# Normalising attention by a reciprocal row read back from memory instead of a broadcast made on TensorE

## The chip, the cores and the metric

The kernel runs on one core of a Trainium2 chip. The metric is the device time of one execution in microseconds (us); of several runs the median is given. PE is TensorE, DVE is VectorE, ACT is ScalarE, POOL is GpSimd and SP is SyncE, whose queue issues all transfers of this kernel.

## What is computed

One inference step of a two-layer backbone. Layer 0 runs multi-head latent attention beside a convolution branch; layer 1 is a bidirectional Mamba-2 mixer. Two groups of tokens go through both: 256 context tokens, which see only themselves, and 1024 latent tokens, which see 512 cached context tokens and all 1024 latent ones. The change touches attention alone, and of it the last steps:

```python
s = (einsum('bqhd,bkhd->bhqk', qn, k_nope) + einsum('bqhr,bkr->bhqk', qr, k_rope)) * ATTN_SCALE
p = softmax(s, axis=-1)
out = einsum('bhqk,bkhd->bqhd', p, v)          # 8 heads, 64 wide each
...
mix = concatenate([attn, cv], axis=-1) * silu(gate)
return mix @ w_out, ckv, k_rope
```

The kernel leaves softmax unnormalised until the values are multiplied, so it owes each query a factor 1/(sum of its exponentials), beside the gate.

## The kernel before

Attention runs by **units** (p, b, j, qi): p is one of 4 pairs of heads, b one of 5 blocks of 256 queries (b=0 is context with 256 keys, b=1 to 4 are latent with 1536 keys), j the head of the pair, qi the half of the block (128 queries). 80 units follow each other in that order; four units with the same (p, b) are called a **group** here, 20 in all, numbered 0 to 19, and units are numbered 0 to 79.

For each unit `u_scores` makes 128 x 1536 scores on PE into three PSUM banks (tile `pss`, three float32r products for each, lines 119 to 121), takes their row maximum on DVE (`mx`, `nm`, lines 617 and 621), and exponentiates on ACT (`prob`, line 626), which also leaves the sums. DVE adds the sums and takes the reciprocal, one column of 128 numbers (`ri`, lines 630, 631 and 633). `u_trans`, called one unit later, transposes `prob` on PE, four blocks of 128 x 128 to a bank (`pspt`, line 646), and copies them to `ptile` on ACT (line 652) or DVE (line 650). When a group's four units are through, `u_values` multiplies values by `ptile` into one PSUM bank (`pspo`, line 666), head j=0 into partitions 0 to 63 and j=1 into 64 to 127. A unit has 3 x 3 matmuls of scores, 12 transposes, and a quarter of 24 matmuls of values (for b=0: 3, 2, and a quarter of 4).

The reciprocal has one number per query, and queries lie along the free side of `pspo`; it must reach all 64 partitions of its head. Before, PE did that: a matmul of `ri`, repeated over 64 columns, with the identity puts the row into the right half of the same bank, four such matmuls a group (line 661). DVE then makes the gate times that row (`t2`, line 671, printed as `t` in the profile) and the product with the values (`om`, line 672), and SP stores `om` to memory (`mixd`, line 673). The gate `sg` is loaded from memory (line 705), two buffers.

A scheduler orders each engine's instructions after the program is recorded, so what is written in one function may stand among instructions of other units; each engine, SP too, runs its own list strictly in order. Between the units stand the normalisation of the convolution branch (`conv_norm`) and the keys and queries of the next pair (`prep_pair`, after units 19, 39 and 59). From unit 68 on, `load_mix` reads `mixd` back (line 690) and splits it on ACT (line 691) and DVE (line 692) into `hl` for the output projection, eight rows of heads k in the order 4, 5, 6, 7, 0, 1, 2, 3. Row k=3 needs the last pair's blocks b=0 to 2, that is group 17. The output projection (tile `psmm`) follows the last group.

Of the kernel before, what the change touches and what calls it, by code (L numbers as in the profile page):

```python
# [10 lines left out]
F32 = mybir.dt.float32  # L11
# [3 lines left out]
AF = mybir.ActivationFunctionType  # L15
# [35 lines left out]
def body(nc, tc, d, dbg=None, stop=None):  # L51
    es = ExitStack()
    with es:
        _body(nc, tc, d, es, dbg or {}, stop)


def _body(nc, tc, d, es, dbg, stop):
    V, S, G, PE = nc.vector, nc.scalar, nc.gpsimd, nc.tensor
    dma = nc.sync.dma_start

    def pool(name, bufs=1, space=None, side=None, stack=es):
        kw = {}
        if space is not None:
            kw["space"] = space
        if side is not None:
            kw["side"] = side
        if space is None:
            kw["reuse_waits"] = "tile"
        return stack.enter_context(tc.tile_pool(name=name, bufs=bufs, **kw))
# [5 lines left out]
    sm = pool("sm", bufs=3, side="left")  # L75
# [9 lines left out]
    dp = pool("dp", space=DRAM)  # L85

    def psum(tag="x"):
        tag = tag if tag in ptags else "sd"
        p, n = ptags[tag]
        return p.tile([128, 512], F32, name="ps" + tag, tag=tag, bufs=n)  # L90
# [5 lines left out]
    ident = cp.tile([128, 128], F32, name="ident")  # L96
# [21 lines left out]
    def mm3(ps, lh, ll, rh, rl, start, stop_):  # L118
        PE.matmul(ps, lh, rh, start=start, stop=False)  # L119
        PE.matmul(ps, lh, rl, start=False, stop=False)  # L120
        PE.matmul(ps, ll, rh, start=False, stop=stop_)  # L121

    def after(ins, other):
        tc.add_manual_dep(ins.ins, other.ins.name,
                          mybir.DependencyInfo(mybir.DependencyClass.Sync, mybir.DependencyReason.DATA), reason="group")
# [56 lines left out]
    def bcast_cols(r, j0, jn, ps):  # L182
        for j in range(jn):
            PE.matmul(ps[:, j * 128:(j + 1) * 128], r[:, j0 + j:j0 + j + 1].to_broadcast([128, 128]), ident,
                      start=True, stop=True)
        return ps
# [246 lines left out]
    for c0, n in CHUNKS:  # L433
        ps = psum()
# [65 lines left out]
    ap_ = pool("attn", bufs=2, side="right", stack=esB)  # L500
# [20 lines left out]
    for c0, n in CHUNKS:  # L521
        ps = bcast_cols(rq, c0 // 128, n // 128, ps=psum("pt"))
# [69 lines left out]
    units = []  # L592
    for p in range(4):
        for b in range(5):
            for j in range(2):
                for qi in range(2):
                    units.append((p, b, j, qi))

    def u_scores(u, kq):
        p, b, j, qi = u  # L600
        ks, qs = kq
        tok = (0 if b == 0 else 256 + 256 * (b - 1)) + 128 * qi
        ci = 0 if tok < 256 else (1 if tok < 768 else 2)
        o = tok - CHUNKS[ci][0]
        segs = [0] if b == 0 else [1, 2, 3]
        qh, ql = qs[(j, ci)]
        mx = sm.tile([128, 4], F32, name="mx", tag="mx", bufs=6)
        sums = sm.tile([128, 4], F32, name="sums", tag="sums", bufs=6)
        nk = sum(KSEG[si][1] for si in segs)
        prob = ap_.tile([128, 1536], F32, name="prob", tag="prob")  # L610
        pss = []
        for x, si in enumerate(segs):
            n = KSEG[si][1]
            kh, kl = ks[(j, si)]
            ps = psum("s")
            mm3(ps[:, :n], qh[:, o:o + 128], ql[:, o:o + 128], kh[:, :n], kl[:, :n], True, True)
            V.tensor_reduce(mx[:, x:x + 1], ps[:, :n], axis=AX.X, op=ALU.max, negate=len(segs) == 1)  # L617
            pss.append((ps, n))
        if len(segs) > 1:
            nm = sm.tile([128, 1], F32, name="nm", tag="nm", bufs=6)  # L620
            V.tensor_reduce(nm, mx[:, :len(segs)], axis=AX.X, op=ALU.max, negate=True)  # L621
        else:
            nm = mx[:, 0:1]
        c = 0
        for x, (ps, n) in enumerate(pss):
            S.activation(prob[:, c:c + n], ps[:, :n], AF.Exp, bias=nm, accum_out=sums[:, x:x + 1])  # L626
            c += n
        ri = sm.tile([128, 1], F32, name="ri", tag="ri", bufs=8)
        if len(segs) > 1:
            V.tensor_reduce(ri, sums[:, :len(segs)], axis=AX.X, op=ALU.add)  # L630
            V.reciprocal(ri, ri)
        else:
            V.reciprocal(ri, sums[:, 0:1])
        return prob, ri, nk

    def u_trans(u, st, pts):
        p, b, j, qi = u
        prob, ri, nk = st
        for g in range(0, nk // 128, 4):
            n4 = min(4, nk // 128 - g)  # L640
            if qi == 0:
                pts[(j, g)] = ap_.tile([128, 4, 256], F32, name="ptile", tag="pt", bufs=7)
            dst = pts[(j, g)]
            ps = psum("pt")
            for x in range(n4):
                PE.transpose(ps[:, x * 128:(x + 1) * 128], prob[:, (g + x) * 128:(g + x + 1) * 128], ident)  # L646
            o = dst[:, :n4, qi * 128:qi * 128 + 128]
            p3 = ps[:, :n4 * 128].rearrange("p (k q) -> p k q", q=128)
            if g == 4:
                V.tensor_copy(o, p3)  # L650
            else:
                S.copy(o, p3)  # L652
        pts[("r", j, qi)] = ri

    def u_values(p, b, pts):
        q0 = 0 if b == 0 else 256 + 256 * (b - 1)
        kts = list(range(2)) if b == 0 else list(range(2, 14))
        po = psum("po")
        for qi in range(2):
            for j in range(2):  # L660
                PE.matmul(po[64 * j:64 * j + 64, 256 + 128 * qi:384 + 128 * qi],
                          pts[("r", j, qi)].to_broadcast([128, 64]), ident, start=True, stop=True)
        for x, kt in enumerate(kts):
            for j in range(2):
                h = 2 * p + j
                PE.matmul(po[64 * j:64 * j + 64, 0:256], vt[:, kt, 64 * h:64 * h + 64],  # L666
                          pts[(j, 4 * (x // 4))][:, x % 4, :], start=x == 0, stop=x == len(kts) - 1)
        t2 = ap_.tile([128, 256], F32, name="t2", tag="t2")
        sg = sgs.pop((p, b))
        om = ap_.tile([128, 256], F32, name="om", tag="om")  # L670
        V.tensor_mul(t2, sg, po[:, 256:512])
        V.tensor_mul(om, po[:, 0:256], t2)
        dma(mixd[p, :, q0:q0 + 256], om)

    KORD = (4, 5, 6, 7, 0, 1, 2, 3)
# [9 lines left out]
    def load_mix(gi, ks):  # L685
        g0, gn, _ = GRP[gi]
        for k in ks:
            hi = gtile(gi, "hl", F32R, p=hls[gi])
            lo = gtile(gi, "hl", F32R, p=hls[gi])
            dma(f32(lo), mixd[k, :, g0:g0 + gn])  # L690
            S.copy(hi, f32(lo))
            V.tensor_sub(lo, f32(lo), f32(hi))
            mix[gi][0][k], mix[gi][1][k] = [(g0, hi)], [(g0, lo)]
# [1 line left out]
    state = {}  # L695
    kqs = {0: prep_pair(0)}
    done, ci, sgs = {}, 0, {}
    late_v = []
    cn = [st for t0 in range(0, T, 256) for st in [conv_norm(t0)] * 5]
    for i in range(len(units) + 2):  # L700
        if i < len(units):
            u = units[i]
            if i % 4 == 0:
                sgs[u[:2]] = ap_.tile([128, 256], F32, name="sg", tag="sg")
                dma(sgs[u[:2]], sgd[u[0], :, 256 * u[1]:256 * u[1] + 256])
            state[u] = u_scores(u, kqs[u[0]])
            if i % 20 == 19 and u[0] < 3:
                kqs[u[0] + 1] = prep_pair(u[0] + 1)
        if 0 < i <= len(units):
            v = units[i - 1]  # L710
            pts = done.setdefault((v[0], v[1]), {})
            u_trans(v, state.pop(v), pts)
            if v[2] == 1 and v[3] == 1:
                late_v.append(v)
        if i % 4 == 1 and late_v:
            v = late_v.pop(0)
            u_values(v[0], v[1], done.pop((v[0], v[1])))
        if ci < len(cn) and i % 20 in (1, 3, 5, 7, 9, 11, 13):
            next(cn[ci])
            ci += 1  # L720
        if i == 68:
            esE.close()
            esA.close()
            wps[0] = pool("wpB", bufs=2, side="left")
            hls.append(pool("hlB0", bufs=16, side="left", stack=esH))
            load_mix(0, KORD[:4])
            wao.extend(split_w(d["wao"][m], 8, 128) for m in range(2))
    assert ci == len(cn)
    esB.close()
    esP.close()  # L730
    dump("mix", mixd.rearrange("a p t -> (a p) t"))
# [157 lines left out]
    def dtile(name, dt=F32, tag=None):  # L889
        return dq.tile([128, HT], dt, name=name, tag=tag or name)  # L890
# [40 lines left out]
    p = dtile("p")  # L931
# [43 lines left out]
    for half in range(2):  # L975
        hs = slice(half * 64, half * 64 + 64)
        for c0 in range(0, 5):
            c = half * 5 + c0
            ps = psum("sd")
# [560 lines left out]
```

## Time and profile before

| | |
|---|---|
| three runs | 2059.69, 2059.83, 2062.99 us (median 2059.83) |
| profiled execution, its own time | 2060.95 us |
| its span | 2059.1 us |
| PE busy over the span | 1993.4 us (97%) |
| DVE busy | 1415.9 us (69%) |
| ACT busy | 882.3 us (43%) |
| attention's units | about 380 to 797 us |

The page's busy shares are averages over stages with different limits, so the stage of attention is read by itself: how busy each engine is in stretches of it, which instructions follow each other on PE and at what distance, and which waits stand at the place where the change puts new ones. Times in the views are counted from the start of the span.

### The profile page before, as it was taken

What the parts mean: (1) busy time and instruction counts of PE and PEld (TensorE: products, weight loads), DVE (VectorE), ACT (ScalarE), POOL (GpSimd) and SP (SyncE); (2) the same over time, 40 slices, a digit from 0 to 9 for tenths busy, and PEclk for the clock granted to TensorE, in tenths of its full rate; (3) what the DMA queues carried; (4) which work ended last, traced back from release to release, by engine and by line L of the source; (5) the groups of instructions that cost most, each with busy time, mean ns of one, the idle gap of its engine ahead of it and who ended that gap; (6) DMA issues with size and microseconds to landing.
All of it is one profiled execution on the core that took longest, in us unless ns stands there. A gap on an engine that the chain in (4) does not pass through costs nothing.

```text
span 2059.1 us, 32474 instructions
## 1 busy us (share of the span) xinstructions
PE 1993.4 (97%) x11830; PEld 1626.0 (79%) x11830; DVE 1415.9 (69%) x2257; ACT 882.3 (43%) x1683; POOL 578.7 (28%) x487
## 2 busy tenths in 40 slices
PE   6999999999999999989999999999999999799997
PEld 3787888777777777868888888888888888589997
DVE  5798798556666673275757876876778587784744
ACT  5411321666566673244544343443334244333531
POOL 1211122212222311563123333333433243342001
PEclk8999999999999999999999999999999999999998
DMA  8434213311122224331566768765866678755442
GB/s 315 181 118 150 54 70 108 115 57 42 57 60 60 77 82 164 140 114 52 142 217 205 229 203 237 208 191 173 244 204 194 179 235 252 220 182 185 145 157 72
DMA packets 273341, 313.57 MB, mean 152 GB/s; under 512 B 21184, under 2 KB 221920, under 8 KB 273184
## 3 DMA queue, kind: packets, MB, share of 16 engines
q1 hardware_dynamic: 273184, 311.51, 48.0%
q8 instruction: 94, 1.54, 0.3%
q14 instruction: 63, 0.52, 0.1%
HBM read 223.38 MB, written 88.05 MB: 151 GB/s over the span
## 4 chain that ended last, share of the span: by engine, by line
PE 90%; DVE 3%; DMA 2%; ACT 1%; issue 1%; SPq 1%; POOL 0%; DVEq 0%; ACTq 0%; POOLq 0%
PE psmm L119 18%; PE psmm L120 18%; PE psmm L121 18%; PE pspo L666 5%; PE pspt L646 4%; PE pssd L1078 3%; PE pss L119 3%; PE pssd L1159 3%; PE pss L121 3%; PE pss L120 3%; PE pssd L1164 2%; PE pssd L1136 2%; PE pssd L1139 2%; PE psx L229 1%; PE pstm L1036 1%
## 5 line engine op out<-in xcount | busy, mean ns | idle before, releaser
L119 PE MATMUL psmm<-hl,wh 128*128 128x512 f32 (+1 forms) x1152 | 428.1, 372 | 4.7 <-ACT wh L114 3.5
L121 PE MATMUL psmm<-hl,wl 128*128 128x512 f32 (+1 forms) x1152 | 423.5, 368 | 4.3 <-POOL wl L115 4.3
L120 PE MATMUL psmm<-hl,wh 128*128 128x512 f32 (+1 forms) x1152 | 423.3, 367 | 0.0
L115 POOL TENSOR_TENSOR wl<-ws,wh 128x1024 fp32r<-128x1024 f32 x89 | 223.6, 2514 | 516.7 <-ACT wh L114 424.5
L119 PEld LDWEIGHTS psmm<-hl,wh 128*128 128x128 f32 x1152 | 219.1, 190 | 37.6 <-ACT wh L114 4.5
L121 PEld LDWEIGHTS psmm<-hl,wl 128*128 128x128 f32 x1152 | 218.8, 190 | 36.9 <-POOL wl L115 6.2
L120 PEld LDWEIGHTS psmm<-hl,wh 128*128 128x128 f32 x1152 | 218.8, 190 | 29.6 <-issue 0.7
L383 DVE SCALAR_TENSOR_TENSOR cacc<-cvin,acw,cacc 128x1295 f32<-128x1295 f32 x120 | 206.9, 1740 | 4.6 <-ACT cacc L378 3.1
L114 ACT CAST wh<-ws 128x1024 fp32r<-128x1024 f32 x109 | 113.6, 1043 | 199.6 <-PE psmm L120 140.3
L848 DVE SCALAR_TENSOR_TENSOR cy<-raw,prm,cy 128x1282 f32<-128x1282 f32 x96 | 157.2, 1637 | 24.6 <-ACT cy L845 17.0
L120 PE MATMUL psmm<-hlo,wh 128*128 128x512 f32 (+3 forms) x480 | 172.1, 359 | 0.0
L119 PE MATMUL psmm<-hh,wh 128*128 128x512 f32 (+3 forms) x480 | 167.8, 360 | 2.5 <-ACT hh L259 2.0
L121 PE MATMUL psmm<-hh,wl 128*128 128x512 f32 (+3 forms) x480 | 170.1, 357 | 0.0
L617 DVE TENSOR_REDUCE mx<-pss 128x1 f32<-128x512 f32 (+1 forms) x208 | 137.3, 668 | 35.2 <-PE pss L121 34.2
L1083 POOL TENSOR_TENSOR st<-st,dec_bc 128x256 f32<-128x256 f32 x104 | 84.3, 815 | 245.2 <-DVE st L1085 165.9
L119 PE MATMUL psmm<-yh,wh 128*128 128x256 f32 (+1 forms) x476 | 147.8, 314 | 5.2 <-ACT yh L1203 3.1
L120 PE MATMUL psmm<-yl,wh 128*128 128x256 f32 (+1 forms) x476 | 148.0, 312 | 0.4 <-DVE yl L1204 0.4
L121 PE MATMUL psmm<-yh,wl 128*128 128x256 f32 (+1 forms) x476 | 147.1, 313 | 0.0
L626 ACT ACTIVATE prob<-pss,nm 128x512 f32<-128x512 f32 x192 | 130.3, 693 | 16.1 <-DVE nm L621 14.2
L646 PE MATMUL pspt<-ident,prob 128*128 128x128 f32 x800 | 121.7, 278 | 4.9 <-ACT prob L626 3.9
L652 ACT COPY ptile<-pspt 128x512 f32<-128x512 f32 (+1 forms) x144 | 81.2, 569 | 104.8 <-PE pspt L646 104.0
L646 PEld LDWEIGHTS pspt<-ident,prob 128*128 128x128 f32 x800 | 92.1, 141 | 40.4 <-ACT prob L626 10.2
(337 smaller groups left out, 4084.5 us busy)
## 6 DMA issues: line engine op xcount, KB each, us to landing
xa<-cmb SPq DMA_DIRECT2D x80, 384.0 KB
wm<-in_wmod_dram SPq DMA_DIRECT2D x48, 512.0 KB
ws<-in_wc_dram SPq DMA_DIRECT2D x40, 512.0 KB
eb<-eyd SPq DMA_DIRECT2D x160, 128.0 KB
ws<-in_wco_dram SPq DMA_DIRECT2D x32, 512.0 KB
cmb<-xt SPq DMA_DIRECT2D x24, 640.0 KB
bx<-cmb SPq DMA_DIRECT2D x72, 192.0 KB
eb<-cmb SPq DMA_DIRECT2D x80, 128.0 KB
```

The source lines that it names most:

```text
L114: S.copy(wh, ws)
L115: (eng or G).tensor_sub(wl, ws, f32(wh))
L119: PE.matmul(ps, lh, rh, start=start, stop=False)
L120: PE.matmul(ps, lh, rl, start=False, stop=False)
L121: PE.matmul(ps, ll, rh, start=False, stop=stop_)
L383: V.scalar_tensor_tensor(cacc[i], cv[:, k:k + CO], acw[:, 31 * i + k:31 * i + k + 1], cacc[i], ALU.mult, ALU.add)
L617: V.tensor_reduce(mx[:, x:x + 1], ps[:, :n], axis=AX.X, op=ALU.max, negate=len(segs) == 1)
L626: S.activation(prob[:, c:c + n], ps[:, :n], AF.Exp, bias=nm, accum_out=sums[:, x:x + 1])
L646: PE.transpose(ps[:, x * 128:(x + 1) * 128], prob[:, (g + x) * 128:(g + x + 1) * 128], ident)
L666: PE.matmul(po[64 * j:64 * j + 64, 0:256], vt[:, kt, 64 * h:64 * h + 64], pts[(j, 4 * (x // 4))][:, x % 4, :], start=x == 0, stop=x == len ...
L848: V.scalar_tensor_tensor(y, raw[:, k:k + RO], ccw[:, 5 * blk + k:5 * blk + k + 1], y, ALU.mult, ALU.add)
L1083: G.tensor_mul(n.rearrange("p (h e) -> p h e", e=64), s.rearrange("p (h e) -> p h e", e=64), dec_ap(u, dr, c))
```

## The change

PE's four matmuls a group with the identity go, and so does the product of gate and row. In their place:

- the four reciprocals of a group go into the four columns of one tile `ri` [128, 4], and after the fourth unit SP stores it to memory, to a row of `rid` [20, 4, 128], transposed by the store's addresses (2 KB, in runs of one number of 4 bytes);
- `u_values` multiplies the values in PSUM by the gate and leaves the product in `om` (three buffers instead of two);
- at the first unit of the next group but one (unit 4g+8 for group g) `row_load` reads the row back, twice, once for each head, each time repeated to 64 partitions (`rb`, two buffers); a dependency makes it wait for the last exponential recorded by then, that of unit 4g+8;
- two units later `row_scale` multiplies `om` by `rb` on DVE, and SP stores `om` to `mixd`.

```diff
+    rgs, late_o, last_exp = {}, deque(), []
+    rid = dp.tile([20, 4, 128], F32, name="rid")
...
-        ri = sm.tile([128, 1], F32, name="ri", tag="ri", bufs=8)
+        if (j, qi) == (0, 0):
+            rgs[p, b] = sm.tile([128, 4], F32, name="ri", tag="ri", bufs=4)
+        ri = rgs[p, b][:, 2 * j + qi:2 * j + qi + 1]
...
-        return prob, ri, nk
+        last_exp[:] = [ex]
+        if (j, qi) == (1, 1):
+            dma(rid[5 * p + b].rearrange("c q -> q c"), rgs.pop((p, b)))
+        return prob, nk, mx
...
-        for qi in range(2):
-            for j in range(2):
-                PE.matmul(po[64 * j:64 * j + 64, 256 + 128 * qi:384 + 128 * qi],
-                          pts[("r", j, qi)].to_broadcast([128, 64]), ident, start=True, stop=True)
...
-        V.tensor_mul(t2, sg, po[:, 256:512])
-        V.tensor_mul(om, po[:, 0:256], t2)
+        om = ap_.tile([128, 256], F32, name="om", tag="om", bufs=3)
+        V.tensor_mul(om, po[:, 0:256], sgs.pop((p, b)))
+        late_o.append((p, b, q0, om))
+
+    def row_load(it):
+        rb = ap_.tile([128, 256], F32, name="rb", tag="rb")
+        for x in range(2):
+            ld = dma(rb[64 * x:64 * x + 64], rid[5 * it[0] + it[1], 2 * x:2 * x + 2].rearrange("c q -> (c q)")
+                     .unsqueeze(0).to_broadcast([64, 256]))
+            if last_exp:
+                after(ld, last_exp[-1])
+        return rb
+
+    def row_scale(it, rb):
+        p, b, q0, om = it
+        V.tensor_mul(om, om, rb)
         dma(mixd[p, :, q0:q0 + 256], om)
...
-    for i in range(len(units) + 2):
+    for i in range(len(units) + 7):
...
+        if i % 4 == 0 and late_o:
+            rows_.append((late_o[0], row_load(late_o.popleft())))
+        if i % 4 == 2 and rows_:
+            row_scale(*rows_.popleft())
```

Three places show what the scheduler makes of it. The first is PE in the middle of attention, around units 13 and 14 (`prob_3517` and `prob_3506` are unit 13 before and now, `prob_3600` and `prob_3581` unit 14). Before:

```order
L646 MATMUL pspt_3630<-ident_63,prob_3517 128x128 x4
L661 MATMUL pspo_3782<-ident_63,ri_3494 64x128
L646 MATMUL pspt_3636<-ident_63,prob_3517 128x128 x4
L119 MATMUL pss_3655<-kh_2861,qh_2951 128x512
...
L121 MATMUL pss_3699<-kh_2839,ql_2907 128x512
L661 MATMUL pspo_3782<-ident_63,ri_3621 64x128
L661 MATMUL pspo_3782<-ident_63,ri_3538 64x128
L646 MATMUL pspt_3676<-ident_63,prob_3600 128x128 x4
L646 MATMUL pspt_3683<-ident_63,prob_3600 128x128 x4
```

Now:

```order
L654 MATMUL pspt_3610<-ident_63,prob_3506 128x128 x4
L654 MATMUL pspt_3616<-ident_63,prob_3506 128x128 x4
L669 MATMUL pspo_3766<-ptile_3529,vt_2713 64x256
L119 MATMUL pss_3637<-kh_2862,qh_2952 128x512
...
L121 MATMUL pss_3681<-kh_2840,ql_2908 128x512
L654 MATMUL pspt_3651<-ident_63,prob_3581 128x128 x4
L654 MATMUL pspt_3658<-ident_63,prob_3581 128x128 x4
```

The 64-column matmuls of line 661 that stood alone between transposes and scores are gone; a single one of the values (line 669 now) has come forward to stand alone in one such place. Counted over all of attention, stretches of 64-column matmuls between other work on PE go from 109 (37 of them of line 661 alone) to 74.

The second is DVE around the sums of unit 28 (`ri_4425` before, `sums_4373` now; `sums_4420` is unit 29). Before:

```order
L630 TENSOR_REDUCE ri_4425<-sums_4403 128x1
L617 TENSOR_REDUCE mx_4529<-pss_4532 128x1
L621 TENSOR_REDUCE nm_4464<-mx_4446 128x1
L631 RECIPROCAL ri_4425<-ri_4425 128x1
L617 TENSOR_REDUCE mx_4529<-pss_4537 128x1
L630 TENSOR_REDUCE ri_4469<-sums_4447 128x1
```

Now:

```order
L635 TENSOR_REDUCE ri_4395<-sums_4373 128x1
L620 TENSOR_REDUCE mx_4494<-pss_4497 128x1
L624 TENSOR_REDUCE nm_4437<-mx_4419 128x1
L636 RECIPROCAL ri_4395<-ri_4395 128x1
L620 TENSOR_REDUCE mx_4494<-pss_4502 128x1
L686 TENSOR_TENSOR om_4258<-om_4258,rb_4416 128x256
L635 TENSOR_REDUCE ri_4395<-sums_4420 128x1
```

The product with the loaded row of group 5 has come in between, behind the second maximum of unit 30 and ahead of the sums of unit 29; its load waits for the exponential of unit 28.

The third is ACT near the end of attention, at the split of row k=3 of `mixd` (`hl_7514` before, `hl_7435` now). Before, it stood behind unit 74's exponentials (`prob_7125`):

```order
L626 ACTIVATE prob_7125,sums_7124<-pss_7136,nm_7141 128x512
L652 COPY ptile_7082<-pspt_7161 128x4x128
L691 CAST hl_7514<-hl_7515 128x768
L652 COPY ptile_7193<-pspt_7194 128x4x128
L626 ACTIVATE prob_7169,sums_7168<-pss_7170,nm_7185 128x512
```

Now it stands behind unit 77's (`prob_7187`) and ahead of unit 78's (`prob_7260`):

```order
L629 ACTIVATE prob_7187,sums_7186<-pss_7198,nm_7203 128x512
L705 CAST hl_7435<-hl_7436 128x768
L660 COPY ptile_7224<-pspt_7225 128x4x128
L660 COPY ptile_7210<-pspt_7283 128x4x128
L629 ACTIVATE prob_7260,sums_7259<-pss_7261,nm_7276 128x512
```

It has moved three units later, with the store of group 17 that its load reads.

## Rows read from the trace of the kernel before

**Rows 1.** Stretches of attention: length, then busy PE, PEld, DVE, ACT, POOL, then clock.

```profile
440.00:500.00 60.00, 59.19 (x374) 41.88 (x373) 35.82 (x77) 33.18 (x83) 14.18 (x14) 1.00 0.26 75
740.00:790.00 50.00, 48.65 (x320) 34.66 (x320) 35.42 (x77) 36.75 (x89) 0.06 (x1) 1.00 0.24 82
```

**Rows 2.** Chain that ended last, 430 to 470 us, by line.

```profile
by line: PE pspo L666 30.2%; PE pspt L646 27.4%; PE pss L119 14.3%; PE pss L121 12.3%; PE pss L120 12.1%; PE pspo L661 4.0%; issue 0.1%
```

**Rows 3.** Groups by shape, 360 to 830 us: count, busy us, mean ns, idle before.

```profile
L666 PE MATMUL pspo<-ptile,vt 128*64 128x256 f32 x800 | 111.5, 386 | 0.0
...
L661 PE MATMUL pspo<-ident,ri 128*64 128x128 f32 x160 | 25.4, 297 | 0.7 <-DVE ri L631 0.7
...
L671 DVE TENSOR_TENSOR t<-sg,pspo 128x256 f32<-128x256 f32 x20 | 8.4, 421 | 34.7 <-PE pspo L666 34.7
```

**Rows 4.** PE's instructions in order of time, 446 to 466 us: start, duration, line.

```profile
446.91 0.60 PE L646 MATMUL pspt<-ident,prob 128*128 128x128 f32 x4
447.44 0.43 PE L661 MATMUL pspo<-ident,ri 128*64 128x128 f32 x2
447.80 0.66 PE L646 MATMUL pspt<-ident,prob 128*128 128x128 f32 x4
448.21 0.48 PE L119 MATMUL pss<-kh,qh 128*128 128x512 f32 x1
...
450.91 0.44 PE L661 MATMUL pspo<-ident,ri 128*64 128x128 f32 x4
451.28 1.09 PE L646 MATMUL pspt<-ident,prob 128*128 128x128 f32 x8
452.13 0.48 PE L119 MATMUL pss<-kh,qh 128*128 128x512 f32 x1
...
461.94 2.38 PE L666 MATMUL pspo<-ptile,vt 128*64 128x256 f32 x20
464.25 0.66 PE L646 MATMUL pspt<-ident,prob 128*128 128x128 f32 x4
464.83 0.65 PE L666 MATMUL pspo<-ptile,vt 128*64 128x256 f32 x2
465.41 0.50 PE L119 MATMUL pss<-kh,qh 128*128 128x512 f32 x1
```

**Rows 5.** ACT and DVE around the last exponential of unit 28, in order of time.

```profile
518.23 0.25 ACT L626 ACTIVATION_READ_ACCUMULATOR prob<-pss,nm 128x1 f32 x1
...
520.29 0.67 DVE L617 TENSOR_REDUCE mx<-pss 128x1 f32<-128x512 f32 x1
523.31 0.16 DVE L630 TENSOR_REDUCE ri<-sums 128x1 f32<-128x3 f32 x1 [2.35 <-ACT prob L626]
```

**Rows 6.** Store of group 17, load of row k=3 and its split, in order of time.

```profile
758.77 0.34 SPq L673 DMA_DIRECT2D mixd<-om  x1
...
760.75 0.32 SPq L690 DMA_DIRECT2D hl<-mixd  x1
...
764.21 0.87 ACT L691 CAST hl<-hl 128x768 fp32r<-128x768 f32 x1
```

**Rows 7.** Units 76 to 78 on ACT and DVE, in order of time.

```profile
771.01 0.22 ACT L626 ACTIVATION_READ_ACCUMULATOR prob<-pss,nm 128x1 f32 x1
...
773.70 1.38 DVE L617 TENSOR_REDUCE mx<-pss 128x1 f32<-128x512 f32 x2 [2.08 <-PE pss L121]
...
777.21 0.22 ACT L626 ACTIVATION_READ_ACCUMULATOR prob<-pss,nm 128x1 f32 x1
...
782.46 0.69 ACT L626 ACTIVATE prob<-pss,nm 128x512 f32<-128x512 f32 x1
```

**Rows 8.** End of attention, in order of time.

```profile
788.71 0.16 DVE L631 RECIPROCAL ri<-ri 128x1 f32<-128x1 f32 x1
...
796.42 0.42 DVE L672 TENSOR_TENSOR om<-pspo,t 128x256 f32<-128x256 f32 x1
...
796.99 0.36 PE L119 MATMUL psmm<-hl,wh 128*128 128x256 f32 x1 [1.06 <-DVE raw L813]
```

More of the change, by code (lines that the diff above doesn't have):

```diff
@@ L625, in u_scores @@
         for x, (ps, n) in enumerate(pss):
-            S.activation(prob[:, c:c + n], ps[:, :n], AF.Exp, bias=nm, accum_out=sums[:, x:x + 1])
+            ex = S.activation(prob[:, c:c + n], ps[:, :n], AF.Exp, bias=nm, accum_out=sums[:, x:x + 1])
             c += n
-        ri = sm.tile([128, 1], F32, name="ri", tag="ri", bufs=8)
+        if (j, qi) == (0, 0):
+            rgs[p, b] = sm.tile([128, 4], F32, name="ri", tag="ri", bufs=4)
+        ri = rgs[p, b][:, 2 * j + qi:2 * j + qi + 1]
         if len(segs) > 1:
@@ L633, in u_scores @@
             V.reciprocal(ri, sums[:, 0:1])
-        return prob, ri, nk
+        last_exp[:] = [ex]
+        if (j, qi) == (1, 1):
+            dma(rid[5 * p + b].rearrange("c q -> q c"), rgs.pop((p, b)))
+        return prob, nk, mx
     def u_trans(u, st, pts):
         p, b, j, qi = u
-        prob, ri, nk = st
+        prob, nk, _ = st
         for g in range(0, nk // 128, 4):
@@ L652, in u_trans @@
                 S.copy(o, p3)
-        pts[("r", j, qi)] = ri
     def u_values(p, b, pts):
@@ L667, in u_values @@
                           pts[(j, 4 * (x // 4))][:, x % 4, :], start=x == 0, stop=x == len(kts) - 1)
-        t2 = ap_.tile([128, 256], F32, name="t2", tag="t2")
-        sg = sgs.pop((p, b))
-        om = ap_.tile([128, 256], F32, name="om", tag="om")
-        V.tensor_mul(t2, sg, po[:, 256:512])
-        V.tensor_mul(om, po[:, 0:256], t2)
+        om = ap_.tile([128, 256], F32, name="om", tag="om", bufs=3)
[12 more added lines that the diff above has]
+        V.tensor_mul(om, om, rb)
         dma(mixd[p, :, q0:q0 + 256], om)
@@ L697, in _body @@
     done, ci, sgs = {}, 0, {}
-    late_v = []
+    late_v, rows_ = [], deque()
     cn = [st for t0 in range(0, T, 256) for st in [conv_norm(t0)] * 5]
-    for i in range(len(units) + 2):
+    for i in range(len(units) + 7):
         if i < len(units):
@@ L727, in _body @@
             wao.extend(split_w(d["wao"][m], 8, 128) for m in range(2))
-    assert ci == len(cn)
+    assert ci == len(cn) and not late_o and not rows_
     esB.close()
```

## The prediction

> **What bounds the kernel now.** I read the stage first by stretches [rows 1]. In the middle of attention PE is busy 59.19 of 60 us at full clock (the row's 1.00), DVE 35.82 and ACT 33.18; near the end PE has 48.65 of 50. No other engine is near its limit, and PE hardly waits. The chain of waits from 430 to 470 us says the same in another way [rows 2]: every step is PE's own instruction following another one of PE, and line 661 has 4.0% of it. So this stage costs what PE's instructions take from start to start, and I price removed work by these distances, not by durations, which overlap.
>
> The group table shows why durations would mislead [rows 3]: line 661 has 160 instructions (80 matmuls, two each) of 297 ns, 25.4 us busy, but two of them that run beside each other need far less. The same table says that DVE's first product waits 34.7 us in 20 times for PE's last values. DVE is thus late for nobody there; it waits for PE.
>
> **What line 661 costs on PE.** In [rows 4] one matmul of line 661 stands between two times four transposes and then scores: from 446.91 to 448.21 is 1.30 us. Eight transposes in one piece and then scores take 451.28 to 452.13, 0.85 us. That makes 0.45 us for one excursion. Two matmuls in one excursion take 0.37 us (450.91 to 451.28), one takes 0.36 (447.44 to 447.80): the second is nearly free. Coming in costs as well: the four transposes ahead of it take 0.53 us (446.91 to 447.44) where eight take 0.85, that is 0.42 for four. And the first eight transposes behind an excursion are themselves a little slow, so I take 0.48 us each.
>
> In the order of the program there are 37 excursions of line 661 alone (20 with one matmul, 17 with two). They go: 37 x 0.48 = 17.8 us. Of the other 26 matmuls, those that stand with a single matmul of the values run beside it and cost nothing; three places with three of them in front of values cost about 0.36 us each: 1.1 us. Together 18.9 us.
>
> Against that, the values are cut up a little more. Ten matmuls of values take 2.31 us (461.94 to 464.25), one takes 0.58 (464.83 to 465.41) [rows 4]: 0.43 for each two, head by head side by side, plus 0.15 for leaving, and about 0.10 for coming in. There are 74 excursions with values where there were 72 (0.5 us), and because more of them have an odd number, 225 pairs instead of 222 (1.3 us). PE's gain is 18.9 - 1.8 = 17.1 us.
>
> **What comes in its place, on DVE.** The two products on DVE stay two: gate times values reads PSUM as before (0.42 us, [rows 3]), the product with the loaded row reads SBUF. No row has that one alone with this shape; I take 0.42 as well, and between 0.2 and 0.5 it changes nothing, since DVE has 24 us idle in 60.
>
> The question is the wait for `rb`. The load is held back until the last exponential of unit 4g+8 and the product stands on DVE five instructions behind that unit's sums. For group 5 I can put times to it from [rows 5]: ACT ends unit 28 at 518.48. SP then issues two loads at 0.32 us each, and the second lands about 1.98 us after its issue (the nearest row is a store and the load that waited for it, 758.77 to 760.75 [rows 6]; these loads move half as much each). That is about 521.1 to 521.4. DVE has done the second maximum of unit 30 at 520.96, so it waits 0.2 to 0.4 us and multiplies until 521.8; its next instruction waits for unit 29's exponential until 523.31 anyway, with 2.35 us idle before it in the row. The product falls into that hole. The other groups have the same order on DVE; in the three at a change of pairs, where the units are short, the product stands one unit later. I charge 1 us in all for places where a copy or a maximum stands right behind the product; 0 to 6 for the range.
>
> On SP the store of reciprocals and the two loads wait for DVE and ACT, and loads of keys for the next pair, of gates, and stores of `mixd` queue behind them. The keys are wanted only after four short units, and the gates four units later. I charge nothing; if a load of keys did come late, it would hold PE for a few us at each of three changes of pairs.
>
> The store of the reciprocals consists of numbers of 4 bytes, and no row shows such a store; only the last group waits for it. There the reciprocal is done at 788.87, and the product with the row is wanted at 796.84, when DVE's last product of before ends [rows 8]. With 0.32 and 0.64 us of issuing and 1.98 us for the loads, the store may take up to 5 us before it is late. I take 2 to 4: hidden. Were it late, the output projection would still have three PSUM banks to fill before it needs DVE. The Trainium skill speaks against this store ("DMA: Bandwidth & Descriptors", rules for kernel authors): a transfer whose last dimension is not contiguous is cut into one descriptor for each element, here 512. No run so far shows the price; by it the sum would only change if the store took over 5 us.
>
> PE's first matmul of the projection waits for the release of the values' bank, two products after the last values before, one now: 0.42 us gained [rows 8].
>
> **What the later store costs.** Row k=3 of the mixed input needs the store of group 17, now behind the product at unit 77's maxima instead of right behind its values. At the times of [rows 7] that product ends at about 775.5 (the two maxima end at 775.08). Store 1.98 us and load up to 3.46 us, as in [rows 6], give 780.9. ACT has finished unit 77 at 777.43, and the split stands next in its list: it is idle for 3.5 us, where it would have copied transposes. The split ends at 781.8, DVE's half of it at 782.8; three maxima of 0.69 us come behind that, so unit 78's exponential starts at about 785 instead of 782.46. PE has transposes of unit 77 and scores of 79 to do meanwhile, so not all of it is lost: 2 us, between 0 and 3.
>
> **Sum.** -17.1 (PE) + 1.0 (DVE's waits) + 2.0 (row k=3) - 0.4 (bank) = -14.5 us. The profiled execution took 2060.95 us, 1.1 above the median of the runs: 2046.5 for the profile, 2045.4 in medians. I forecast 2045.5, and 2042 to 2050 for this case.
>
> **Rivals.** (a) The freed time turns into bubbles. PE's list is 4% shorter, but a unit's loop of maximum, exponential, copy and transposes is not, and the scheduler has placed it anew. For it: near the end PE already waits a little [rows 1]. Against it: DVE and ACT have 40% idle. If a unit lost 0.1 us on average, 8 us would go: 2053 (2050 to 2058).
> (b) DVE's wait for `rb` is the new bound. It is one mechanism at one place: the list of DVE, with maxima and copies behind the product. It decides when the row lands later than the next sums are due, 4.8 us after the exponential in [rows 5] instead of my 2.6 to 2.9; SP held up by another wait would do it. If then 18 groups lost 1.5 us each on PE, 27 us would eat the gain: 2060 - 17 + 27 = 2070, slower.
> (c) PE is not the bound; its modelled ends only hide waiting, and then removed matmuls save nothing: 2060. Against it stand the even distances of [rows 4] and a chain without any other engine [rows 2]. The Trainium skill ("Perfetto Trace Analysis", Identifying the Most-Contended Engine) calls a matmul's busy share no good measure and wants that of the weight loads, which is 70% here (41.88 of 60 in [rows 1]); by that rule there would be room on PE, and this rival is what it would give.
> (d) The excursions cost more than I take and the split of k=3 is hidden: -17.1 - 0.4 - 2 = -19.5, 2040.
>
> **How the numbers follow.** Forecast 0.62, (a) 0.16, (b) 0.07, (c) 0.07, (d) 0.08. The range goes down to 2039 for (d) and up to 2056 for most of (a); outside are (b), (c) and the ends, under 2 in 10. About 0.2% (4.1 us) is what a measurement of this kernel tells from no change. Faster by more than that: the forecast, (d), and two thirds of (a), 0.81. Within it: a third of (a) and most of (c), 0.11. Slower: (b) and a rest, 0.08.
>
> **What would show it.** In the profile of after: no line with `ident,ri`; attention's stage from 380 to about 782 instead of 797 us; PE still above 97% busy in its middle; the product with `rb` preceded by less than 0.5 us of waiting for a DMA in most groups; a wait of ACT for the load of `hl` of some 3 us near the end. I would be wrong if DVE shows over 1 us of waiting for `rb` in many groups, if PE's wait for `prob` grows by several us, or if the split of k=3 holds ACT for much longer.

## The result, and the profile after

The changed kernel takes 2095.7 us (median; 2089.7 to 2098.0), the kernel before, beside it, 2061.4. The ratio is 1.0163, with a 95% interval of 1.0147 to 1.0178: 34 us slower, where 15 us faster was forecast, and outside the range. The profiled execution has a span of 2094.1 us.

The loss lies in attention. From its first scores to the first matmul of the output projection it takes 447.5 us instead of 415.3. Stretches of the kernel after, with columns as in [rows 1]:

```profile
440.00:500.00 60.00, 57.77 (x348) 41.67 (x345) 38.00 (x87) 35.82 (x91) 13.96 (x13) 1.00 0.37 74
740.00:790.00 50.00, 43.93 (x264) 30.67 (x263) 29.66 (x66) 30.55 (x71) 7.13 (x3) 0.93 0.37 82
790.00:830.00 40.00, 33.88 (x208) 23.61 (x207) 16.46 (x42) 17.95 (x46) 0.00 (x0) 0.89 0.08 20
```

In the middle PE has lost 1.4 of 60 us against [rows 1], near the end 4.7 of 50, and there the granted clock is 0.93 instead of 1.00. The chain of waits from 430 to 470 us, which had only PE in [rows 2], now has the load of the row as its largest line ("DMA rb<-rid 21.5%"). Some of the waits from 375 to 850 us (engine and line, what it waited for, us in total, times, longest):

```profile
DVE om L686 <- DMA rb<-rid: 76.1, 19, 7.9
ACT hl L705 <- DMA hl<-mixd: 33.4, 6, 17.8
ACT prob L629 <- DVE nm L624: 24.5, 13, 4.3
PEld pss L119 <- ACT prob L629: 20.6, 33, 2.4
PE pss L119 <- ACT prob L629: 9.9, 13, 2.1
DVE om L672 <- PE pspo L669: 6.3, 8, 1.3
```

DVE hardly waits for PE's values any more (34.7 us in [rows 3], 6.3 now). It waits 76.1 us for the loaded row instead, 19 times 4 us on average, and ACT and PE wait behind it. Of the 33.4 us of `hl` only 11.1 lie inside attention (up to 830 us); the rest, with the longest wait, belongs to splits behind attention, where the kernel before waits as well (22.2 us in the same stretch, none of it inside attention). At the product of group 5, which the prediction worked out from [rows 5], SP and DVE show this (start, us, engine and line, what, idle before):

```profile
519.86 0.37 SPq L641 DMA_DIRECT2D rid<-ri  x1
522.36 1.09 SPq L678 DMA_DIRECT2D rb<-rid  x2
...
528.57 0.43 DVE L686 TENSOR_TENSOR om<-om,rb 128x256 f32<-128x256 f32 x1 [4.00 <-DMA rb<-rid]
```

The store at 519.86 is the one of the *next* group, 6. The trace's semaphore events give a landing for each transfer (from its issue to the last increment): this store lands at 528.1, 8.3 us after its issue, and the loads of group 5's row, issued 2.5 us behind it, at 528.5. Over the 20 groups the store takes 8.3 us (median; 7.9 to 10.7) for 2 KB, and the loads 5.9 (2.4 to 9.7). All loads under 2.8 us but one had no store in flight; that one was issued 0.5 us ahead of a store.

The end of attention shows the same, with the projection waiting for it:

```profile
819.30 0.54 SPq L641 DMA_DIRECT2D rid<-ri  x1
...
827.59 0.43 DVE L686 TENSOR_TENSOR om<-om,rb 128x256 f32<-128x256 f32 x1 [6.94 <-DMA rb<-rid]
827.93 0.42 DVE L672 TENSOR_TENSOR om<-pspo,sg 128x256 f32<-128x256 f32 x1
...
828.40 0.58 PE L119 MATMUL psmm<-hl,wh 128*128 128x256 f32 x1 [2.67 <-DVE om L672]
```

The product of group 18 (827.59) stands ahead of the one that gives the values' bank free (827.93), so the projection starts at 828.40 instead of 796.99 [rows 8].

### The profile page after: what moved, and what is told of

The parts are those of the page before. It is cut to its first block, busy times and chain, and to the rows that moved or that the text cites. A ratio compares the mean times of both kernels' runs of the same rounds, so it can differ in the third digit from the quotient of the medians.

```text
span 2094.1 us, 32255 instructions
## 1 busy us (share of the span) xinstructions
PE 2000.8 (96%) x11670; PEld 1630.5 (78%) x11670; DVE 1409.5 (67%) x2257; ACT 883.2 (42%) x1683; POOL 581.9 (28%) x487
## 4 chain that ended last, share of the span: by engine, by line
PE 85%; DMA 6%; DVE 4%; ACT 3%; issue 1%; SPq 0%; POOL 0%; DVEq 0%; ACTq 0%; POOLq 0%
PE psmm L119 18%; PE psmm L120 18%; PE psmm L121 18%; PE pspo L669 3%; DMA rb<-rid 3%; PE pssd L1096 3%; PE pspt L654 3%; PE pssd L1177 3%; PE pss L119 3%; PE pss L120 2%; PE pss L121 2%; PE pssd L1182 2%; PE pssd L1154 2%; PE pssd L1157 2%; ACT prob L629 1%; PE psx L229 1%
## 5 line engine op out<-in xcount | busy, mean ns | idle before, releaser
L654 PEld LDWEIGHTS pspt<-ident,prob 128*128 128x128 f32 x800 | 96.7, 145 | 57.9 <-ACT ptile L660 12.4
```

## The experiments

**Theories.** Q: the store in 512 pieces of 4 bytes takes 8 us, and what is issued around it lands late. D: the dependency on the last exponential makes the load late. L: the repeated reading is slow. Beside them stands the question of what PE's shorter list is worth: 17 us, or less because the time comes back as waiting (B).

**The store in larger pieces.** Only the addresses in memory change; all engines keep their order.

```diff
-            dma(rid[5 * p + b].rearrange("c q -> q c"), rgs.pop((p, b)))
+            dma(rid[5 * p + b].rearrange("c q -> (c q)").rearrange("(q c) -> q c", c=4), rgs.pop((p, b)))
```

> The changed kernel with the same store in 128 pieces of 16 bytes instead of 512 of 4 bytes; every engine keeps its order of instructions. The rows then hold the reciprocals in another order, so the normalisation is left wrong. Theory Q (the number of pieces sets when the store and what is behind it land): the store lands in 2 to 4 us instead of 8, DVE's wait for rb falls from 76 us to under 20, 2045 to 2058 us. If the delay comes from the way through memory as such, or from the dependency (D), or from the loads (L): the store still takes about 8 us or the wait stays above 50 us, 2085 or more.

Measured: 2056.5 us, 0.9979 of before (0.9967 to 0.9991). The store lands in 1.4 us, the loads in 2.6. The wait for the row in the same stretch:

```profile
DVE om L686 <- DMA rb<-rid: 19.6, 18, 2.8
```

Q holds; D and L fall, since neither the dependency nor the loads were touched. The pieces are worth about 38 us (1.0163 less 0.9979, of 2061). And 19.6 us of waiting for the row are left that cost nothing visible.

The row of the page on packets names the pieces (columns: number, volume, then counts up to a size). After, and with pieces of 16 bytes:

```profile
DMA packets 287102, 316.23 MB, mean 151 GB/s; under 512 B 32384, under 2 KB 235680, under 8 KB 286944
```
```profile
DMA packets 279422, 316.23 MB, mean 154 GB/s; under 512 B 24704, under 2 KB 228000, under 8 KB 279264
```

7680 packets fewer under 512 B is 20 times 512 - 128: one for each number of 4 bytes. By this the trace agrees with the rule that the prediction took from the Trainium skill ("DMA: Bandwidth & Descriptors", rules for kernel authors).

With 256 pieces of 8 bytes:

> The changed kernel with the store in 256 pieces of 8 bytes, each engine's order the same; the rows then hold the reciprocals in another order, so the normalisation is left wrong. If landing goes with the number of pieces (512: 8.3 us, 128: 1.4 us): 3.5 to 5 us, wait for rb 25 to 45 us in all, 2060 to 2075 us. If it is a matter of pieces under some size: either 1.4 us and 2056, or 8 us and 2090.

Measured, one time: 2058.4 us; the store lands in 3.4 us (median), DVE waits 27.1 us for `rb`. Landing rises faster than the pieces: 1.4, 3.4 and 8.3 us for 128, 256 and 512. The time does not follow it: the wait was within what I expected (25 to 45 us), and the time, one run, was below it (2060 to 2075) and hardly above that with 16 bytes. Number and size of the pieces change together here, so which of the two counts was not told apart.

**The load ahead of the next store.**

```diff
-        if i % 4 == 0 and late_o:
+        if i % 4 == 0 and rows_:
+            row_scale(*rows_.popleft())
+        if i % 4 == 2 and late_o:
             rows_.append((late_o[0], row_load(late_o.popleft())))
-        if i % 4 == 2 and rows_:
-            row_scale(*rows_.popleft())
```

> The changed kernel with the loads of rb two units earlier (at unit 4g+6, ahead of the next group's store of reciprocals at 4g+7) and the product with rb two units earlier too (4g+8), so that load and product stand as far apart as before. Theory Q (the load lands late because it is issued behind the 4-byte store of the next group on the same queue): loads land about 2.5 us after their issue, DVE's wait for rb falls from 76 us in all to under 15, 2045 to 2056 us. Rival D (the dependency on the last exponential and the short distance to the product make the load late): the wait stays above 50 us, 2085 or more. Rival L (the repeated reading itself is slow): the same, 2085 or more. Rival P (the matmuls taken from PE give back nothing): 2060 to 2066 even if the wait goes.

Measured: 2085.2 us, 1.0121 of before (1.0096 to 1.0146). The wait fell to 21.0 us (under 15 expected), the time did not fall with it: my expectation was wrong in what the store does beside. Waits (of those for `hl` 22.6 us lie inside attention), and the places on SP, DVE and ACT that hold what is left:

```profile
ACT hl L705 <- DMA hl<-mixd: 52.8, 7, 17.8
DVE om L686 <- DMA rb<-rid: 21.0, 14, 7.1
...
596.65 1.08 SPq L678 DMA_DIRECT2D rb<-rid  x2
597.78 0.58 SPq L641 DMA_DIRECT2D rid<-ri  x1
...
605.67 0.43 DVE L686 TENSOR_TENSOR om<-om,rb 128x256 f32<-128x256 f32 x1 [7.11 <-DMA rb<-rid]
...
747.49 0.39 SPq L641 DMA_DIRECT2D rid<-ri  x1
747.92 4.11 SPq L704 DMA_DIRECT2D hl<-mixd  x5
...
761.05 0.83 ACT L705 CAST hl<-hl 128x768 fp32r<-128x768 f32 x1 [9.86 <-DMA hl<-mixd]
...
780.59 0.38 SPq L641 DMA_DIRECT2D rid<-ri  x1
781.05 0.46 SPq L704 DMA_DIRECT2D hl<-mixd  x1
...
793.79 0.83 ACT L705 CAST hl<-hl 128x768 fp32r<-128x768 f32 x1 [10.62 <-DMA hl<-mixd]
```

Twice the loads of `hl` are now issued right behind a store, and ACT, with exponentials queued behind its split, stands 10 us. And at 596.65 the two loads of `rb` are issued *ahead* of a store: by the semaphore events the first (1.1 us ahead) lands in 2.5 us, the second (issued at 597.14, 0.6 us ahead) only at 605.57, after 8.4.

**The store alone, on the kernel before** (`ri` as a tile of four columns, and the store, which nothing reads):

```diff
...
+        if (j, qi) == (1, 1):
+            dma(rid[5 * p + b].rearrange("c q -> q c"), rgs.pop((p, b)))
```

> The kernel before with the four reciprocals of a group in one tile and the 4-byte store added, which nothing reads. Theory Q in its wide form (the store holds up every transfer issued in the next 8 to 10 us: gates, keys, mixd, hl): the load of rb ahead of the store left 2085 against 2056.5 with larger pieces, so 2070 to 2089 us here. Narrow form (only the load of rb, for which DVE waits, matters): 2059 to 2064.

Measured: 2079.9 us, 1.0088 of before (1.0060 to 1.0115). The wide form of Q holds: 18 us are lost with no wait for `rb` in the kernel at all. It is lost at two places:

```profile
617.00 0.36 SPq L532 DMA_DIRECT2D ct<-cvd  x1
618.62 0.36 SPq L640 DMA_DIRECT2D rid<-ri  x1
...
626.56 1.26 POOL L535 TENSOR_TENSOR la<-ct 128x512 f32<-128x512 f32 x1 [16.82 <-DMA ct<-cvd]
...
628.67 1.22 PE L539 MATMUL pspt<-la,ones 128*128 128x256 f32 x2 [9.23 <-POOL la L536]
...
756.84 0.37 SPq L640 DMA_DIRECT2D rid<-ri  x1
757.26 2.39 SPq L697 DMA_DIRECT2D hl<-mixd  x5
...
770.93 0.83 ACT L698 CAST hl<-hl 128x768 fp32r<-128x768 f32 x1 [8.84 <-DMA hl<-mixd]
```

Once the normalisation of the convolution branch gets its input late and PE stands in its list for it: the load of 512 KB at 617.00, issued 1.6 us ahead of the store, lands after 9.5 us, where the same load took 3.7 in the kernel before. Once it is a split of `hl` again. At unit 39 this kernel is at 0.0 us from the kernel before (table below), so the other form of `ri` costs nothing by itself up to there.

**The store on a queue of its own** (issued by ACT):

> The changed kernel with the 4-byte store issued by ACT on a queue of its own; loads stay on SP's queue. Theory Q in its first form (what is behind the store on one queue waits its turn): the loads land in about 2.5 us, the wait falls under 20 us, 2047 to 2060 us with 20 issues of ACT more. Theory Q in its second form (the pieces occupy the DMA engines whatever the queue): loads still land after 5 to 10 us, 2080 to 2098. D and L: no change, 2085 to 2098.

Measured: 2092.7 us, 1.0164 of before (1.0138 to 1.0190); DVE waits 91.5 us for `rb`. A queue of its own does not help: the second form, by which the pieces hold up transfers of any queue, is the one that remains. Its reason, that the pieces occupy the DMA engines, is not what the packet records show. For the store at 519.86 of the kernel after, from 519.8 to 521.5 us:

```profile
DMA packets 528, 0.00 MB, mean 1 GB/s; under 512 B 528, under 2 KB 528, under 8 KB 528
```

No packet is recorded from 521.5 to 523.4; the 160 of the two loads lie between 523.4 and 525.3, and from there to 527.9 there is none. Yet the store's increments come from 526.4 to 528.1, and those of the loads just behind them, from 526.5 to 528.5. So as recorded the packets are through early, and the time lies between them and the increments that tell of the landing. What holds those was not shown.

**What PE's term is worth.** The kernel before without line 661 and its product:

```diff
-                PE.matmul(po[64 * j:64 * j + 64, 256 + 128 * qi:384 + 128 * qi],
-                          pts[("r", j, qi)].to_broadcast([128, 64]), ident, start=True, stop=True)
...
-        V.tensor_mul(t2, sg, po[:, 256:512])
-        V.tensor_mul(om, po[:, 0:256], t2)
+        V.tensor_mul(om, po[:, 0:256], sg)
```

> The kernel before without the 80 matmuls of line 661 and without the product of gate and row; the values are scaled by the gate alone, so the normalisation of softmax is left out. It prices PE's term by itself, no DMA is added. The prediction's sum of -17.1 us for PE and -0.4 for the bank: 2041 to 2046 us. Rival P (the time is not PE's): 2057 to 2061.

Measured: 2057.3 us, 0.9988 of before (0.9978 to 0.9998): 2.5 us gained (3.5 by the medians), not 17.5. Attention shrank from 415.3 to 412.5. Adding up the distances from start to start on PE, line 661 had 19.1 us there, as I had priced it. But the distances of all others grew by 16.3 (transposes 8.3, values 3.6, scores 3.3, the rest 1.0), 9 of it time in which no matmul runs at all. PE's waits for `prob`, before and in this kernel:

```profile
PEld pss L119 <- ACT prob L626: 4.6, 12, 0.8
PE pss L119 <- ACT prob L626: 1.3, 4, 0.6
```
```profile
PEld pss L119 <- ACT prob L626: 15.1, 30, 1.5
PE pss L119 <- ACT prob L626: 5.5, 9, 1.0
```

The scores wait for a bank that an exponential still reads. Two runs test whether this is where the gain went: each exponential over half of its columns (0.476 us instead of 0.693, 192 times: 41 us off ACT), once in the kernel before and once without line 661.

```diff
...
-            S.activation(prob[:, c:c + n], ps[:, :n], AF.Exp, bias=nm, accum_out=sums[:, x:x + 1])
+            S.activation(prob[:, c:c + n // 2], ps[:, :n // 2], AF.Exp, bias=nm, accum_out=sums[:, x:x + 1])
...
```

> The kernel before with each exponential over half of its columns (the transposes read the written half twice, the reciprocal is taken of a maximum; attention's output is left wrong). PE's list is as long as before, ACT's is shorter by some 45 us over the 80 units. Theory B (before, PE is full and waits little: 9.5 us of idle in attention): 2051 to 2060 us. If ACT is the bound of before: 2030 or less.

> The kernel before without the row matmuls, and with each exponential over half of its columns, as in the run beside it (attention's output is left wrong). Theory B (without the row matmuls PE waits for banks that ACT's exponentials hold): with the exponentials halved the gain of PE appears, 11 to 17 us under the run beside it. Rival O (the gain is missing because the other order of PE's list costs distance by itself): 2 to 5 us under the run beside it, as with whole exponentials (3.5).

Measured: 2061.5 us (1.0004 of before, 0.9991 to 1.0017) and 2048.2 us (0.9925, 0.9902 to 0.9949). Shorter exponentials give the kernel before nothing (2051 to 2060 was expected, so the first run lies just above it): it *was* bound by PE's list. Without line 661 they bring out 13.4 of the 17.5 us. The waits of the second one:

```profile
PEld pss L119 <- ACT prob L626: 8.2, 21, 1.4
PE pss L119 <- ACT prob L626: 2.0, 2, 1.1
```

So B holds: the list of PE and the loop in which the exponentials stand were nearly equally long, and the other one took over 3 us down the way. These runs shortened the exponentials alone; that maxima and copies belong to that loop is argued, and two runs below bear on it.

**Versions without the loss.** The row by two transposes a group on PE, no DMA:

> The kernel before with the row made by two transposes of 128x128 a group instead of four fp32 matmuls with 64 columns; DVE writes each reciprocal 64 times. No DMA. PE's line 661 costs 19.1 us from start to start in the kernel before; forty transposes at 0.105 us are 4.2. Theory B (time freed on PE comes back as waiting): between the run without any row (2057.3) and before (2060.8): 2056 to 2061. Rival P2 (PE's list sets the time and the run without the row lost its gain to something else): 2044 to 2049.

Measured: 2061.0 us, 0.9989 of before (0.9976 to 1.0001): the same, as B says. The changed kernel with its reciprocals transposed on PE and stored as four pieces of 512 bytes:

```diff
-            dma(rid[5 * p + b].rearrange("c q -> q c"), rgs.pop((p, b)))
+            pass
...
+        PE.transpose(po[0:4, 256:384], rgs.pop((p, b)), ident)
+        r4 = ap_.tile([4, 128], F32, name="r4", tag="r4", bufs=2)
+        S.copy(r4, po[0:4, 256:384])
+        dma(rid[5 * p + b], r4)
```

> The changed kernel with the four columns transposed on PE (one more transpose a group, into the free half of the values' bank), copied by ACT to a tile of 4 x 128 and stored as four pieces of 512 bytes. The result is the reference's. Theory Q (pieces of 4 bytes make the loss): the store lands in under 2.5 us, nothing waits behind it, 2053 to 2060 us, as the run with pieces of 16 bytes (2056.5). Theory B (the time that PE is freed of comes back as waiting for ACT's exponentials and copies): no faster than the run without row matmuls, 2057.3 less 4. If PE's matmuls were worth 17 us after all: 2043 to 2047. If the way through memory costs time whatever the pieces: 2075 or more.

Measured: 2060.2 us, 0.9988 of before (0.9976 to 1.0001): the same. The store lands in 1.2 us. On this kernel, copies of transposes were moved from ACT to DVE (`if g >= 4`, and `if g == 4 or (g == 8 and qi == 1)`, where `if g == 4` stood):

> The kernel with four pieces of 512 bytes, and ACT's second copy of transposes in each latent unit moved to DVE: 64 copies, 64 x 0.594 = 38 us off ACT, 64 x 0.686 = 44 us onto DVE. The result is the reference's. Theory B1 (without the row matmuls ACT's own load holds the banks): the gain of the halved exponentials (45 us off ACT gave 9 to 13) appears here too, 2046 to 2053. Theory B2 (it is the whole chain of maximum, exponential and copy that holds the banks, and a copy moved from ACT to DVE only moves the wait): 2055 to 2066. If DVE becomes the bound: 2070 or more.

> The same with half of these copies moved (those of the second half of a block, 32 copies, 19 us off ACT, 22 onto DVE). B1: about half the gain, 2051 to 2057. B2: 2055 to 2063.

Measured: 2064.1 us (1.0010, 0.9998 to 1.0022) with all of them, 2057.6 (0.9977, 0.9965 to 0.9989) with half. Taking 38 us off ACT by giving DVE 44 brings nothing. That speaks against ACT's load alone (B1, 2046 to 2053 expected) and fits the loop over both engines (B2); a run that shortens DVE's part by itself, which would show it, was not made. The half is faster than before by 4.4 us by the medians and the only version with the whole computation that is faster than both kernels beyond its interval; I had no control of the kernel before with the same copies moved, so which part of it the row's way has stays open.

## Why the prediction was wrong, point by point

How far each kernel is behind the kernel before, from ACT's rows: start of a unit's last exponential, counted from the first exponential, less the same of before (us).

| unit | after | load early | 16 bytes | store alone | no line 661 |
|---|---|---|---|---|---|
| 23 | 0.8 | -1.4 | -1.3 | 0.0 | -1.1 |
| 39 | 10.0 | -2.3 | -1.3 | 0.0 | -2.2 |
| 55 | 13.3 | 2.4 | -1.6 | 12.0 | -3.1 |
| 71 | 20.4 | 2.8 | -1.9 | 12.0 | -3.5 |
| 75 | 27.5 | 13.8 | -1.7 | 20.0 | -2.2 |
| 79 | 32.2 | 21.9 | -1.0 | 19.8 | -2.9 |

**The step that failed first: the store.** The prediction knew that it has 512 pieces, had no row with such a transfer, took 2 to 4 us for it, and wrote "only the last group waits for it". It lands in 8.3 us, and whoever is near it waits: the loads of the group before, `hl`, the input of the convolution branch. "On SP ... I charge nothing" was the same error: I looked at how long SP takes to issue and not at how long what it issued stays in the way. In the sum all of this stood as +1.0 us (DVE's waits); measured are 76.1 us of waiting for the row and, by the run with 16-byte pieces, some 38 us of time. Up to unit 71 the kernel after loses 24 us against the one that only lacks line 661 (20.4 and -3.5), with 58.9 of the 76.1 us of waiting for `rb` in that part; by unit 79 it loses another 11, with splits of `hl` among the causes (7.47 us below). The wait for `rb` that I put at 0.2 to 0.4 us in group 5 was 4.00.

**The step that failed second: PE's term.** -17.1 us was right for the list (19.1 measured for line 661 against 18.9) and wrong for the time: 2.5 to 3.5. "PE hardly waits" in [rows 1, 2] tells that PE's list sets the time now, not how far it may shrink before something else does. The prediction gave rival (a) 8 us for this; 14 was its size (17.5 less 3.5). Even with the store mended the forecast would have been missed by some 11 us (2056.5).

**Rival (b)** named the place, and its point of decision, a row that lands later than 4.8 us after the exponential, was passed: in the kernel after ACT ends unit 28's exponentials at 522.34, and the row lands at 528.5, 6.2 us behind it. The cause that it named, SP held up by another wait, was not the one, and its price of 2070 took PE's 17 us as safe. **Rival (c)** gave 2060 for a list of PE that saves nothing. The runs come near its time (2057.3), for another reason: with shorter exponentials the list does save. The measure that it took from the Trainium skill ("Perfetto Trace Analysis", Identifying the Most-Contended Engine), the busy share of weight loads, said there was room on PE. It came nearer to the time of this edit, but not for its reason: with 41 us less of exponentials the kernel before stayed where it was (2061.5) and went to 2048.2 when line 661 was taken out as well, so PE's list had no room while line 661 was in it.

**Smaller terms.** The product with `rb` was taken as 0.42 us; in most groups it is 0.43 (528.57), the mean in the kernel with 512-byte pieces is 0.60. The loads were taken as 1.98 us by a row of another load [rows 6]; with nothing in the way they take 2.4 to 2.6. Row k=3's split did move behind unit 77 and did hold ACT, as worked out from [rows 7], but for 2.10 us instead of 3.5 (2.03 in the run with 16-byte pieces), and with no store of reciprocals in flight: this term was about right. The split that held ACT longer was that of the second row, behind unit 72, whose load was issued at 765.19, right behind the store at 764.73:

```profile
777.05 0.83 ACT L705 CAST hl<-hl 128x768 fp32r<-128x768 f32 x1 [7.47 <-DMA hl<-mixd]
...
808.98 0.83 ACT L705 CAST hl<-hl 128x768 fp32r<-128x768 f32 x1 [2.10 <-DMA hl<-mixd]
```

The bank's 0.4 us became a wait of 2.67 (828.40). "Were it late, the output projection would still have three PSUM banks to fill" was wrong: the bank that it waited for was the values' own, whose release stood on DVE behind a product with `rb`.

Of the signs named ahead, the missing line with `ident,ri` came true and, nearly, the wait of some 3 us for `hl` (2.10); the others did not. Of the signs of being wrong, "over 1 us of waiting for `rb` in many groups" and "PE's wait for `prob` grows by several us" came true (5.9 us before, 30.5 now, at the scores); "the split of k=3 holds ACT for much longer" did not.

## What to carry to other kernels

A transfer that changes the layout by its addresses is priced by its pieces and by all that is in flight beside it, not by its bytes and not by who reads it: count the pieces, and give the store a layout on the chip first if it needs hundreds of very small ones. Here 20 stores of 512 pieces of 4 bytes cost some 38 us, and with 128 pieces of 16 bytes nothing visible. And before the time of removed work is booked on an engine that is always busy, ask how far the next loop is from it: here 3 us of 17. One run without the work, output aside, tells that before anything is built in its place.

## What the runs showed of the hardware

The landing of 2 KB went from 1.2 us (4 pieces of 512 bytes) and 1.4 (128 of 16) over 3.4 (256 of 8) to 8.3 (512 of 4); each of the last two doublings of the pieces made it 2.4 times as long. The store of 4-byte pieces held up transfers issued behind it, some that were issued ahead of it (by 0.6 us, 597.14 in the run with early loads; by 1.6 us, 617.00 in the run with the store alone, a load of 512 KB), and those of another queue. The packets of the one at 519.86 were all recorded within 1.7 us of its issue; its semaphore increments came 6.5 to 8.3 us after it. In the stretches near the end in which PE lost most to waiting, the granted clock was 0.93 (1.00 in [rows 1] for the same stretch) and 0.89: a part of PE's work behind the waits ran at the lower of its two levels, 1.2 instead of 2.4 GHz. From 776 to 782 us it was 0.57, and PE stood idle for 4.20 us up to its matmul at 778.42. What that part cost by itself was not measured.
